# Row sums of reciprocals: inverse square roots and sums of squares in place of pairs, logarithms and TensorE sums

## The chip, the core and the metric

One core of one Trainium2 chip runs the kernel. The time is in device microseconds (us), from one execution of the program; a lower time is better. The kernel before has three runs: 167.90, 168.17 and 172.02 us, median 168.17 us. The profile is of one execution of its own, whose span from the first to the last instruction is 166.3 us.

Engines are named as the profile names them: PE is TensorE (PEld its weight loads), DVE is VectorE, ACT is ScalarE, POOL is GpSimd and SP is SyncE, which here only issues transfers.

## The reference

```python
"x": np.abs(np.random.randn(32, 512, 1024)).astype(np.float32) + 1e-6
...
def reference(x):
    return np.sum(1.0 / x, axis=-1).astype(np.float32)
```

There are 16,384 rows of 1,024 positive float32 numbers, 67.1 MB in all. Each row gives one number, the sum of the reciprocals of its elements.

## The kernel before

The rows are laid over 128 partitions, so that each partition has 128 rows of 1,024 elements. In what follows a "row" is one such row on all 128 partitions at once: 512 KB of input, 128 x 1024 elements. `ring` holds 40 rows in SBUF; row r lies in place r % 40. All loads go from SP's queue into `ring` (line 187). A load of n rows is one transfer, which lands as a whole for whoever waits for it, unless it wraps around the ring's end, where it is cut in two. SP issues the loads in order, and each waits until the rows that lay in its places before have been read for the last time.

The work uses 1/a + 1/b = (a + b) / (ab). A row is cut into two halves a and b of 512 elements. Their products go to `prod` (22 places of 512 elements):

- `P`, line 199: POOL multiplies the halves of one or two rows.
- `C` (line 209) and `V` (line 220): PE copies half b into a PSUM bank by a product with the identity matrix, and DVE multiplies half a by it. `W` (line 220 too) is the same product with both halves in SBUF.
- `L`, line 242, and `E`, line 251: ACT takes the logarithm of the product and then exp of minus that, which is 1/(ab). These two passes over half as many elements make about one pass over all of them. The result goes to a PSUM bank (`ps`) for some rows and stays in `prod` for others.
- `S`, line 232: for those others PE adds the halves, a + b, into a PSUM bank.
- `R`, line 267: DVE multiplies 1/(ab) by the sum, or by the whole row where PE made none, and sums the result along the row into `sums`. This is one instruction of 512 or of 1,024 elements and a short read of the accumulator.

The last two rows, 126 and 127, are loaded and worked on as four pieces of 512 elements.

The order of everything is a list written out by hand, `PLAN` (lines 38 to 73). A token is an operation, a row, a number of rows (`P0+2`), and a bank or place (`@3`); `D10` loads the next ten rows. The loop goes through the list and gives each token to its engine, so every engine has its own queue in the order of the list, and waits come only from the data. `note` drops waits that others imply. The first loads are `D2 D10 D14 D14`, and later ones become smaller down to single rows. The results leave in six small stores once the first 114 rows are done (line 289), and one store for the rest (line 291).

Of the kernel before, what the change touches and what calls it, by code (L numbers as in the profile page):

```python
# [11 lines left out]
def kernel(  # L12
# [5 lines left out]
    nc = tc.nc  # L18
    f32 = mybir.dt.float32
    P = 128  # L20
    D = 1024
    H = D // 2
    F = 128
    R = 40
    NP = 22
    LAST = F - 2
    DONE = 114
    S = float(2**17)

# [6 lines left out]
        D2 D10 D14 D14 P0+2 C3@3 S2@0 V3 P2 L0+2@0 C11@3 S3@1 E0+2@6 P4+2 V11 L2+2@2 R0 S6@2  # L39
        E2+2 R1 P6+2 L4+2@4 R2 R3 E4+2@6 S7@0 P8+2 L6+2@8 R4 S10@1 E6+2 R5 P10 L8+2@10 R6 R7  # L40
        S11@2 E8+2@6 L10+2@6 R8 E10+2 R9 D11 R10 R11 P12+2 C19@3 S14@0 V19 P14+2 L12+2@12
        S15@1 E12+2@6 S18@2 R12 P16+2 L14+2@16 R13 E14+2 R14 P18 L16+2@18 R15 S19@0 E16+2@6
        P20+2 L18+2@14 R16 S22@1 E18+2 R17 D9 P22+2 L20+2@20 R18 R19 E20+2@6 S23@2 P24+2
        L22+2@0 R20 E22+2 R21 L24+2@2 R22 R23 E24+2@6 P26 C27@3 R24 S26@0 P28+2 V27 R25 D7
        L26+2@4 C35@3 E26+2 S27@1 P30+2 V35 L28+2@8 R26 S30@2 R27 E28+2@6 P32+2 L30+2@10 R28
        S31@0 E30+2 R29 P34 L32+2@12 S34@1 R30 R31 E32+2@6 P36+2 S35@0 L34+2@6 R32 E34+2 R33
        D7 P38+2 S38@2 L36+2@16 R34 R35 E36+2@6 S39@1 P40+2 L38+2@18 R36 C43@3 E38+2 R37 D6
        S42@0 P42 L40+2@14 V43 R38 E40+2@6 P44+2 R39 S43@2 L42+2@20 R40 E42+2 S46@1 R41 D3
        P46+2 L44+2@0 R42 R43 E44+2@6 S47@0 P48+2 L46+2@2 R44 S50@2 E46+2 R45 P50 L48+2@4
        R46 C51@3 R47 E48+2@6 S51@1 P52+2 V51 R48 D6 L50+2@8 C59@3 E50+2 R49 P54+2 S54@0  # L50
        L52+2@10 V59 R50 E52+2@6 R51 S55@2 P56+2 L54+2@12 R52 E54+2 S58@1 R53 D5 P58
        L56+2@16 R54 R55 E56+2@6 S59@0 P60+2 L58+2@6 R56 S62@2 E58+2 R57 D4 P62+2 L60+2@14
        R58 R59 E60+2@6 S63@1 P64+2 L62+2@18 R60 S66@0 E62+2 R61 D4 P66 L64+2@20 R62 C67@3
        R63 E64+2@6 P68+2 S67@2 V67 R64 L66+2@0 S70@1 R65 D4 E66+2 P70+2 L68+2@2 R66 R67
        S71@0 E68+2@6 P72+2 L70+2@4 R68 D3 E70+2 R69 D2 C75@3 P74 L72+2@10 S74@2 R70 V75
        P76+2 E72+2@6 R71 S75@1 L74+2@8 R72 D2 E74+2 R73 D2 P80 S78@0 L76+2@12 R74 P81
        L80@16 R75 S79@2 E76+2@6 P78+2 L81@17 R76 D2 S81@1 E80@5 E81 R80 L78+2@6 W82 E78+2
        R81 R77 D1 D1 D1 D1 D1 P88 C85@6 S85@1 R78 P83 L88@18 V85 E88@7 R79 P84 S84@0
        L82+2@14 R88 E82+2@5 P86+2 L84+2@19 R82 D1 E84+2 R83 D1 D1 D1 C90@7 P91 L86+2@0
        S91@2 R85 P93 V90 E86+2@5 R84 P92 S90@1 L90+2@2 R87 L93@21 W89 L92@10 R86 D1 D1 D1  # L60
        D1 E93@7 P94 S97@0 E92@6 R93 E90+2 P97 S94@3 L89@11 R92 E89@7 P95 L97@8 R91 S95@4
        E97 R90 L94+2@4 W96 R97 P101 C99@6 L96@9 R89 E94+2 S100@0 P98 V99 E96@5 L101@12 R95
        P100 S99@1 L98@13 R96 E101@7 L99+2@16 R101 E98@6 P104 C103@5 R94 E99+2 S105@2 R98
        P102 L104@18 V103 E104@7 W105 L102+2@6 R100 P107+2 C106@6 L105@14 R104 E102+2@4
        S108@0 V106 E105 R102 L106+3@19 P109 S107@3 R103 P110 E106+3 R105 S106@4 R99 P111+2
        L109+2@0 R107 S112@1 R108 E109+2@6 R106 L111+2@10 P114 R109 S111@0 E111+2 R110 P113
        L114@15 R111 C115@7 P116 L113@2 R112 E114@6 V115 E113@5 S117@0 P117 R114 L116@3
        L115@8 P118 E116@7 R113 S118@1 E115@6 P119 L117+2@12 R116 E117+2 R115 P120 S120@2
        L119@9 R117 P121 L120@4 S121@3 R118 E119@7 E120 R119 P122 L121@5 S122@0 E121 R120
        P123 L122@18 R121 E122 W124 L123@6 R122 L124@7 W125 S125@1 E123@7 E124@6 R123 P126  # L70
        L125@14 P127 L126@16 S127@0 R124 E125 P128 L127@17 S128@2 E126@7 P129 R125 E127
        S129@3 L128@19 R126 L129@20 E128 R127 E129 R128 R129
    """.split()

    Ln = mybir.ActivationFunctionType.Ln
    Exp = mybir.ActivationFunctionType.Exp
# [10 lines left out]
            act_func_set_id=act_sets.index("natural_log_exp_and_others"),  # L87
# [6 lines left out]
    pspool = ctx.enter_context(  # L94
        tc.tile_pool(name="pspool", bufs=1, space=bass.MemoryType.PSUM)
    )
    ring = pool.tile([P, R, D], f32)
    prod = pool.tile([P, NP, H], f32)
    sums = pool.tile([P, F], f32)
    ident = pool.tile([P, P], f32)  # L100
    ps = pspool.tile([P, 8, H], f32)
    make_identity(nc, ident)

    def parse(tok):
        body, _, b = tok[1:].partition("@")
        r, _, n = body.partition("+")
        return tok[0], int(r), int(n or 1), int(b) if b else None

    ops = [parse(tok) for tok in PLAN]

    pslot = {r + j: b + j for op, r, n, b in ops if op == "L" for j in range(n)}

    def place(r):
        if r < LAST:
            return r, 0, H
        part, q = divmod(r - LAST, F - LAST)
        return LAST + q, part * H, H // 2

    def xs(r, h):
        q, at, w = place(r)  # L120
        return ring[:, q % R, at + h * w : at + (h + 1) * w]

    loaded = 0
    left = set(range(DONE))
    bank, copied, halves, summed = {}, {}, set(), set()

# [36 lines left out]
    def rows(r, n, h=None):  # L166
        spaces = []
        for q, at, w in (place(i) for i in range(r, r + n)):
            end = at + 2 * w
            if h is not None:  # L170
                at, end = at + h * w, at + (h + 1) * w
            spaces += [("row", q % R, i) for i in range(at, end, H // 2)]
        return spaces

    def slots(r, n):
        return [("slot", pslot[q]) for q in range(r, r + n)]

    with tc.manual_schedule():
        for op, r, n, b in ops:
            p = pslot.get(r)  # L180
            if op == "D":
                n, r = r, loaded
                while n:
                    q, at, w = place(r)
                    a = q % R
                    m = min(n, R - a, LAST - r) if r < LAST else 1
                    inst = nc.sync.dma_start(  # L187
                        out=ring[:, a : a + m, at : at + 2 * w],
                        in_=x_v[:, q : q + m, at : at + 2 * w],
                    )  # L190
                    note("SP", inst, writes=rows(r, m))
                    r, n = r + m, n - m
                loaded = r
            elif op == "P":
                while n:
                    q, at, w = place(r)
                    a, p = q % R, pslot[r]
                    m = min(n, R - a)
                    inst = nc.gpsimd.tensor_tensor(  # L199
                        out=prod[:, p : p + m, :w],  # L200
                        in0=ring[:, a : a + m, at : at + w],
                        in1=ring[:, a : a + m, at + w : at + 2 * w],
                        op=mult,
                    )
                    note("POOL", inst, rows(r, m), slots(r, m))
                    r, n = r + m, n - m
            elif op == "C":
                copied[r] = b
                inst = nc.tensor.matmul(  # L209
                    ps[:, b, : place(r)[2]],  # L210
                    lhsT=ident,
                    rhs=xs(r, 1),
                    start=True,
                    stop=True,
                )
                note("PE", inst, rows(r, 1, 1), [("bank", b)])
            elif op in "WV":
                w = place(r)[2]
                in1 = xs(r, 1) if op == "W" else ps[:, copied[r], :w]
                inst = nc.vector.tensor_tensor(  # L220
                    out=prod[:, p, :w], in0=xs(r, 0), in1=in1, op=mult
                )
                if op == "W":
                    read = rows(r, 1)
                else:
                    read = rows(r, 1, 0) + [("bank", copied[r])]
                note("DVE", inst, read, slots(r, 1))
            elif op == "S":
                bank[r] = b
                halves.add(r)  # L230
                for h in range(2):
                    inst = nc.tensor.matmul(  # L232
                        ps[:, b, : place(r)[2]],
                        lhsT=ident,
                        rhs=xs(r, h),
                        start=h == 0,
                        stop=h == 1,
# [84 lines left out]
```

## Time and profile before

| what | value |
|---|---|
| median of three runs | 168.17 us |
| profiled execution, span | 166.3 us |
| median less span | 1.87 us |
| busy, share of the span: PE, DVE, ACT, POOL | 80%, 77%, 80%, 77% |
| loads: bytes read, mean rate over the span | 67.11 MB, 404 GB/s |
| last store issued | 164.06 us |
| ACT's table load, once | 1.28 us |

The time of a run is the span and a little around it. The busy time of an engine says how much of the span it had an instruction running, not whether the kernel waited for it. The profile's chain shows, going back from the last instruction, what each step waited for. "Pitch" is used below for the distance from the start of one instruction to the start of the next on the same engine; where the next one doesn't wait for anything, the pitch is a little shorter than the duration of one, because instructions overlap at their ends.

### The profile page before, as it was taken

What the parts mean: (1) busy time and instruction counts of PE and PEld (TensorE: products, weight loads), DVE (VectorE), ACT (ScalarE), POOL (GpSimd) and SP (SyncE); (2) the same over time, 40 slices, a digit from 0 to 9 for tenths busy, and PEclk for the clock granted to TensorE, in tenths of its full rate; (3) what the DMA queues carried; (4) which work ended last, traced back from release to release, by engine and by line L of the source; (5) the groups of instructions that cost most, each with busy time, mean ns of one, the idle gap of its engine ahead of it and who ended that gap; (6) DMA issues with size and microseconds to landing.
All of it is one profiled execution on the core that took longest, in us unless ns stands there. A gap on an engine that the chain in (4) does not pass through costs nothing.

```text
span 166.3 us, 1348 instructions
## 1 busy us (share of the span) xinstructions
PE 132.5 (80%) x292; PEld 55.2 (33%) x292; DVE 128.3 (77%) x282; ACT 132.3 (80%) x157; POOL 128.2 (77%) x81
## 2 busy tenths in 40 slices
PE   0000799978855999999999999988699979989982
PEld 0000333333312444444343433324234424433351
DVE  0000119885787699898998898989899999999994
ACT  3040073949995899999799999996999999999992
POOL 1500795069995999999999999948977869999860
PEclk9999999999996999999999999999999999999999
DMA  5999999999998989999999999999999999999940
GB/s 189 536 394 394 441 441 441 441 441 441 441 441 349 509 368 446 430 417 438 441 434 434 406 426 446 429 424 424 414 437 437 414 410 428 410 409 410 400 139 4
DMA packets 5768, 67.26 MB, mean 404 GB/s; under 512 B 1536, under 2 KB 1536, under 8 KB 3200
## 3 DMA queue, kind: packets, MB, share of 16 engines
q1 hardware_dynamic: 5760, 67.18, 95.6%
q8 instruction: 2, 0.03, 0.1%
q14 instruction: 6, 0.05, 0.1%
HBM read 67.11 MB, written 0.07 MB: 404 GB/s over the span
## 4 chain that ended last, share of the span: by engine, by line
DMA 57%; PE 18%; ACT 8%; DVE 6%; POOL 6%; issue 3%; SPq 1%; ACTq 0%; POOLq 0%; DVEq 0%
DMA ring<-in_x_dram 57%; PE ps L232 15%; POOL prod L199 6%; ACT prod L242 4%; PE ps L209 3%; ACT ps L251 2%; DVE ring L267 2%; DVE prod L267 2%; ACT prod L251 2%; DVE prod L220 1%; SPq L187 1%; DVE sums L267 0%; ACTq L242 0%; POOLq L199 0%; DVEq L317 0%
## 5 line engine op out<-in xcount | busy, mean ns | idle before, releaser
L199 POOL TENSOR_TENSOR prod<-ring 128x1024 f32<-128x1024 f32 (+2 forms) x75 | 127.5, 1727 | 33.5 <-DMA ring<-in_x_dram 27.1
L232 PE MATMUL ps<-ring,ident 128*128 128x512 f32 (+1 forms) x260 | 116.9, 596 | 5.2 <-DVE sums L267 4.5
L242 ACT ACTIVATE prod<-prod 128x1024 f32<-128x1024 f32 (+2 forms) x78 | 68.5, 892 | 24.9 <-DVE prod L220 14.3
L267 DVE CUSTOM_DVE_ANT_1 ring<-ring,ps 128x1024 f32<-128x1024 f32 (+1 forms) x65 | 76.4, 1208 | 8.9 <-ACT ps L251 8.7
L232 PEld LDWEIGHTS ps<-ring,ident 128*128 128x128 f32 x260 | 49.2, 193 | 71.7 <-issue 51.6
L267 DVE CUSTOM_DVE_ANT_0 prod<-prod,ps 128x512 f32<-128x512 f32 (+1 forms) x63 | 40.9, 677 | 0.4 <-PE ps L232 0.4
L209 PE MATMUL ps<-ring,ident 128*128 128x512 f32 x32 | 19.3, 689 | 25.7 <-DMA ring<-in_x_dram 24.0
L251 ACT ACTIVATE ps<-prod 128x1024 f32<-128x1024 f32 (+2 forms) x41 | 34.1, 838 | 4.5 <-DVE sums L267 3.7
L251 ACT ACTIVATE prod<-prod 128x1024 f32<-128x1024 f32 (+3 forms) x37 | 34.4, 931 | 0.9
L220 DVE TENSOR_TENSOR prod<-ring,ps 128x512 f32<-128x512 f32 x16 | 10.9, 684 | 26.3 <-PE ps L209 26.3
L209 PEld LDWEIGHTS ps<-ring,ident 128*128 128x128 f32 x32 | 6.0, 213 | 36.0 <-issue 21.4
L267 DVE DVE_READ_ACCUMULATOR2_ANT sums<- 128x1 f32 x130 | 10.7, 82 | 0.0
L220 DVE TENSOR_TENSOR prod<-ring 128x512 f32<-128x512 f32 x6 | 4.1, 688 | 0.1
L84 ACT ACT_TABLE_LOAD x1 | 1.3, 1283 | 0.7 <-PEq L306 0.7
L267 DVE CUSTOM_DVE_ANT_0 prod<-prod,ps,sums 128x256 f32<-128x256 f32 x2 | 0.9, 475 | 0.0
masks.py:197 POOL MEMSET ident<- 128x128 f32 x1 | 0.2, 204 | 0.3 <-POOLq L306 0.3
masks.py:199 POOL TENSOR_SCALAR_AFFINE_SELECT ident<-ident 128x128 f32<-128x128 f32 x1 | 0.3, 292 | 0.1
L306 POOL MEMSET const-float32-0.0<- 128x1 f32 x1 | 0.1, 98 | 0.2 <-issue 0.2
L306 POOL MEMSET const-bfloat16-1.0<- 128x1 bf16 x1 | 0.1, 101 | 0.0
L306 POOL MEMSET const-uint8-127<- 128x1 uint8 x1 | 0.1, 101 | 0.0
L306 POOL MEMSET const-float32-1.0<- 128x1 f32 x1 | 0.1, 98 | 0.0
## 6 DMA issues: line engine op xcount, KB each, us to landing
ring<-in_x_dram SPq DMA_DIRECT2D x2, 7168.0 KB, 41.2
ring<-in_x_dram SPq DMA_DIRECT2D x2, 3584.0 KB, 29.3
ring<-in_x_dram SPq DMA_DIRECT2D x2, 3072.0 KB, 31.9
ring<-in_x_dram SPq DMA_DIRECT2D x3, 2048.0 KB, 34.0
ring<-in_x_dram SPq DMA_DIRECT2D x1, 5632.0 KB, 30.3
ring<-in_x_dram SPq DMA_DIRECT2D x5, 1024.0 KB, 31.8
ring<-in_x_dram SPq DMA_DIRECT2D x1, 5120.0 KB, 16.5
ring<-in_x_dram SPq DMA_DIRECT2D x1, 4608.0 KB, 30.7
```

Of the source, the lines that this page charges most:

```text
L84: nc.scalar.add_instruction(mybir.InstLoadActFuncSet(name=nc.get_next_instruction_name(), act_func_set_id=act_sets.index("natural_log_exp_ ...
L187: inst = nc.sync.dma_start(out=ring[:, a : a + m, at : at + 2 * w], in_=x_v[:, q : q + m, at : at + 2 * w],)
L199: inst = nc.gpsimd.tensor_tensor(out=prod[:, p : p + m, :w], in0=ring[:, a : a + m, at : at + w], in1=ring[:, a : a + m, at + w : at + 2 * w],
L209: inst = nc.tensor.matmul(ps[:, b, : place(r)[2]], lhsT=ident, rhs=xs(r, 1), start=True, stop=True,)
L220: inst = nc.vector.tensor_tensor(out=prod[:, p, :w], in0=xs(r, 0), in1=in1, op=mult)
L232: inst = nc.tensor.matmul(ps[:, b, : place(r)[2]], lhsT=ident, rhs=xs(r, h), start=h == 0, stop=h == 1,)
L242: inst = nc.scalar.activation(out=pg, in_=pg, func=Ln, scale=S)
L251: inst = nc.scalar.activation(out=rc, in_=pg, func=Exp, scale=-1.0)
L267: inst = nc.vector.tensor_tensor_reduce(out=row, in0=row, in1=other, scale=S, scalar=total if q in summed else 0.0, op0=mult, op1=add, acc ...
L306: nc = _bacc.Bacc("TRN2", target_bir_lowering=False, num_devices=1)
```

## The change

No halves, no pairs and no TensorE are left. ACT computes |x|^-1/2 of whole rows in place in `ring`, in instructions of up to four rows, and the row sum of 1/x is then the sum of the squares of these. The squares are summed in one of four ways:

- `B` (82 rows): VectorE's `bn_stats` on each half row of 512 elements. It gives the mean and a sum of squared deviations (`mean`, `var` in the code) of the even and of the odd elements. `K` later turns these into sums of squares for 32, 32, 32, 22 and 10 rows at once, in four short DVE instructions each.
- `Z` (19 units): ACT's Square with a sum along the row.
- `G` and `T` (26 units): POOL squares the row in place, up to three rows in one instruction, and DVE sums it with `tensor_reduce`.
- `Q` (2 rows): one DVE instruction multiplies the row by itself and sums.

A unit is a row; row 127 is two units of 512 elements, 127 (a `G`, `T` unit) and 128 (a `Z` unit), whose sums one last small DVE addition brings together. `ring` has 48 rows in place of 40. The first loads are of 16, 14 and 13 rows. The first store is of 118 rows, in six parts as before.

```diff
-    R = 40
-    NP = 22
-    LAST = F - 2
-    DONE = 114
-    S = float(2**17)
+    R = 48
+    PIECES = (512, 512)
+    DONE = 118
     PLAN = """
-        D2 D10 D14 D14 P0+2 C3@3 S2@0 V3 P2 L0+2@0 C11@3 S3@1 E0+2@6 P4+2 V11 L2+2@2 R0 S6@2
...
-        S129@3 L128@19 R126 L129@20 E128 R127 E129 R128 R129
+        D16 D14 D13 A0+4 A4+4 B0 Q1 B2 A8+4 G4+3 B3 A12+4 B8 Q9 B10 Z7 G12+3 T4+3 D10 Z15 A16+4
+        B11 A20+4 B16 T12+3 D9 A24+4 G20+3 B17 B18 B19 A28+2 B24 Z23 B25 G28+2 T20+3 D9 A30+4
+        B26 B27 A34+4 T28+2 B30 A38+4 B31 D9 B32 B33 A42 B34 Z37 B35 A43+4 K0+32 B36 D5 B38
+        A47+4 G44+2 B39 B40 B41 Z43 B42 D6 A51+2 T44+2 Z49 B46 D4 A53+4 B47 B48 B50 D4 A57+4 B51
+        B52 B54 Z53 G59 B55 D5 A61 Z60 B56 G61 B57 A62+4 B58 D3 T59 D2 T61 A66+4 G63 K32+32 B64
+        B65 Z62 G69 T63 D3 A70 B66 D3 G70 B67 B68 D2 A71+4 T69 T70 D2 A75+4 B71 B72 D2 B73 D1
+        A79 G75 B74 D1 A80+4 B76 B78 T75 D1 D1 Z77 D1 D1 B79 D1 D1 A84 B80 A85+4 B81 B83 B84 Z82
+        B85 A89+2 B86 A91+4 B87 B88 B89 A95+4 B90 B91 B92 Z96 B93 Z97 B94 A99+4 B95 B98 K64+32
+        A103 B99 A104+3 G103 B101 B102 Z100 T103 G106 A107+2 B104 B105 A109+3 G107 T106 B108
+        Z110 G109 T107 A112+3 B111 T109 A115+2 B112 B113 Z116 B114 A117+2 B115 A119+2 B117
+        K96+22 O0 A121 G119 B120 A122 B121 Z118 B122 A123 T119 A124 B123 A125 G124 A126 B125
+        A127 A128 K118+10 G127 T124 Z126 Z128 T127
     """.split()
...
-            act_func_set_id=act_sets.index("natural_log_exp_and_others"),
+            act_func_set_id=act_sets.index("abs_reciprocal_sqrt_and_small"),
...
+    stats = pool.tile([P, F, 2, 2, 3], f32)
+    part = pool.tile([P, F, 4], f32)
+    total = pool.tile([P, F], f32)
+    sums = pool.tile([P, F + 1], f32)
+    nc.gpsimd.memset(stats, 0.0)
+    nc.gpsimd.memset(sums, 0.0)
...
+            elif op == "A":
+                    inst = nc.scalar.activation(
+                        out=area(u, m), in_=area(u, m), func=Arsqrt, scale=1.0 - 2.0**-17)
...
+            elif op == "Z":
+                inst = nc.scalar.activation(
+                    out=area(u), in_=area(u), func=Square, accum_out=sums[:, c : c + 1])
...
+            elif op == "Q":
+                inst = nc.vector.tensor_tensor_reduce(
+                    out=row, in0=row, in1=row, scale=1.0, scalar=0.0,
+                    op0=mult, op1=add, accum_out=sums[:, u : u + 1])
...
+            elif op == "B":
+                for h in range(0, w, H):
+                    inst = nc.vector.bn_stats(
+                        out=stats[:, r, (at + h) // H],
+                        in_=ring[:, r % R, at + h : at + min(h + H, w)])
...
+            elif op == "G":
+                    inst = nc.gpsimd.tensor_tensor(out=row, in0=row, in1=row, op=mult)
...
+            elif op == "T":
+                    inst = nc.vector.tensor_reduce(
+                        out=sums[:, u : u + m], in_=area(u, m), axis=mybir.AxisListType.X, op=add)
...
+            elif op == "K":
+                nc.vector.tensor_tensor(out=tmp, in0=mean, in1=mean, op=mult)
+                nc.vector.scalar_tensor_tensor(
+                    out=tmp, in0=tmp, scalar=float(H // 2), in1=var, op0=mult, op1=add)
+                nc.vector.tensor_reduce(out=total[:, u : u + n], in_=part[:, u : u + n], axis=mybir.AxisListType.X, op=add)
+                nc.vector.tensor_tensor(
+                    out=sums[:, u : u + n], in0=sums[:, u : u + n], in1=total[:, u : u + n], op=add)
+            elif op == "O":
+                for c in range(0, DONE, DONE // 6):
+                    store(c, min(c + DONE // 6, DONE))
+        nc.vector.tensor_tensor(
+            out=sums[:, F - 1 : F], in0=sums[:, F - 1 : F], in1=sums[:, F : F + 1], op=add)
+        store(DONE, F)
```

More of the change, by code (lines that the diff above doesn't have):

```diff
@@ L7 @@
 from concourse.hw_specs import get_activation_tables
-from concourse.masks import make_identity
 @with_exitstack
@@ L23 @@
     F = 128
-    R = 40
-    NP = 22
-    LAST = F - 2
-    DONE = 114
-    S = float(2**17)
-    PLAN = """
-        D2 D10 D14 D14 P0+2 C3@3 S2@0 V3 P2 L0+2@0 C11@3 S3@1 E0+2@6 P4+2 V11 L2+2@2 R0 S6@2
[L40 to L71, printed above, removed]
-        S129@3 L128@19 R126 L129@20 E128 R127 E129 R128 R129
@@ L73 @@
     """.split()
-    Ln = mybir.ActivationFunctionType.Ln
-    Exp = mybir.ActivationFunctionType.Exp
+    Arsqrt = mybir.ActivationFunctionType.Abs_reciprocal_sqrt
+    Square = mybir.ActivationFunctionType.Square
     mult = mybir.AluOpType.mult
@@ L93, with place, area @@
     pool = ctx.enter_context(tc.tile_pool(name="pool", bufs=1))
-    pspool = ctx.enter_context(
-        tc.tile_pool(name="pspool", bufs=1, space=bass.MemoryType.PSUM)
-    )
     ring = pool.tile([P, R, D], f32)
[L98 to L102, printed above, removed]
-    def parse(tok):
[L105 to L125, printed above, removed]
+    stats = pool.tile([P, F, 2, 2, 3], f32)
[4 more added lines that the diff above has]
+    nc.gpsimd.memset(sums, 0.0)
+    def parse(tok):
+        r, _, n = tok[1:].partition("+")
+        return tok[0], int(r), int(n or 1)
+    def place(u):
+        k = u - (F - 1)
+        if k < 0:
+            return u, 0, D
+        return F - 1, sum(PIECES[:k]), PIECES[k]
+    def area(u, n=1):
+        r, at, w = place(u)
+        return ring[:, r % R : r % R + n, at : at + w]
     history = {}
@@ L164, in note, with rows @@
                 )
-    def rows(r, n, h=None):
+    def rows(u, n=1):
         spaces = []
[L168 to L172, printed above, removed]
-        return spaces
-    def slots(r, n):
-        return [("slot", pslot[q]) for q in range(r, r + n)]
+        for r, at, w in (place(i) for i in range(u, u + n)):
+            spaces += [("row", r % R, i) for i in range(at, at + w, 128)]
+        return spaces
@@ L178, with store @@
+    loaded = 0
+    left = set(range(DONE))
+    def store(lo, hi):
+        nc.sync.dma_start(out=out_v[:, lo:hi], in_=sums[:, lo:hi])
     with tc.manual_schedule():
-        for op, r, n, b in ops:
-            p = pslot.get(r)
+        for op, u, n in (parse(tok) for tok in PLAN):
             if op == "D":
-                n, r = r, loaded
+                n, u = u, loaded
                 while n:
-                    q, at, w = place(r)
-                    a = q % R
-                    m = min(n, R - a, LAST - r) if r < LAST else 1
+                    r, at, w = place(u)
+                    m = min(n, R - r % R, F - 1 - u) if u < F - 1 else 1
@@ L187 @@
                     inst = nc.sync.dma_start(
-                        out=ring[:, a : a + m, at : at + 2 * w],
-                        in_=x_v[:, q : q + m, at : at + 2 * w],
-                    )
[L191 to L194, printed above, removed]
+                        out=area(u, m), in_=x_v[:, r : r + m, at : at + w]
+                    )
+                    note("SP", inst, writes=rows(u, m))
@@ L195 @@
+                    u, n = u + m, n - m
+                loaded = u
+            elif op == "A":
                 while n:
[L196 to L203, printed above, removed]
-                    )
@@ L205 @@
[L205 to L214, printed above, removed]
-                )
[L216 to L237, printed above, removed]
-                    )
-                    note("PE", inst, rows(r, 1, h), [("bank", b)])
-            elif op == "L":
-                pg = prod[:, p : p + n, : place(r)[2]]
-                inst = nc.scalar.activation(out=pg, in_=pg, func=Ln, scale=S)
-                note("ACT", inst, writes=slots(r, n))
-            elif op == "E":
-                pg = prod[:, p : p + n, : place(r)[2]]
-                rc = pg
-                if b is not None:
-                    rc = ps[:, b : b + n, : place(r)[2]]
-                    for j in range(n):
-                        bank[r + j] = b + j
-                inst = nc.scalar.activation(out=rc, in_=pg, func=Exp, scale=-1.0)
-                if b is None:
-                    note("ACT", inst, writes=slots(r, n))
-                else:
-                    banks = [("bank", b + j) for j in range(n)]
-                    note("ACT", inst, slots(r, n), banks)
-            elif op == "R":
-                q, at, w = place(r)
-                other = ps[:, bank[r], :w]
-                if r in halves:
-                    row = prod[:, p, :w]
-                else:
-                    row = ring[:, q % R, at : at + 2 * w]
-                    row = row.rearrange("p (h e) -> p h e", h=2)
-                    other = other.unsqueeze(1).to_broadcast([P, 2, w])
-                total = sums[:, q : q + 1]
@@ new lines @@
+                    m = min(n, R - place(u)[0] % R)
+                    inst = nc.scalar.activation(
+                        out=area(u, m),
+                        in_=area(u, m),
+                        func=Arsqrt,
+                        scale=1.0 - 2.0**-17,
+                    )
+                    note("ACT", inst, writes=rows(u, m))
+                    u, n = u + m, n - m
+            elif op == "Z":
+                c = u - (F - 1) if u >= F else 0
+                c = F if c else u
+                inst = nc.scalar.activation(
+                    out=area(u), in_=area(u), func=Square, accum_out=sums[:, c : c + 1]
+                )
+                note("ACT", inst, writes=rows(u))
+            elif op == "Q":
+                row = area(u)
@@ L269 @@
                     in0=row,
-                    in1=other,
-                    scale=S,
-                    scalar=total if q in summed else 0.0,
+                    in1=row,
+                    scale=1.0,
+                    scalar=0.0,
                     op0=mult,
                     op1=add,
-                    accum_out=total,
+                    accum_out=sums[:, u : u + 1],
                 )
-                summed.add(q)
-                note(
-                    "DVE",
-                    inst,
-                    [("bank", bank[r])],
-                    slots(r, 1) if r in halves else rows(r, 1),
-                )
@@ L285 @@
-                left.discard(r)
-                if not left:
-                    for c in range(0, DONE, DONE // 6):
-                        part = slice(c, min(c + DONE // 6, DONE))
-                        nc.sync.dma_start(out=out_v[:, part], in_=sums[:, part])
-                    left.add(-1)
-        nc.sync.dma_start(out=out_v[:, DONE:], in_=sums[:, DONE:])
+                note("DVE", inst, writes=rows(u))
+            elif op == "B":
+                r, at, w = place(u)
+                for h in range(0, w, H):
+                    inst = nc.vector.bn_stats(
+                        out=stats[:, r, (at + h) // H],
+                        in_=ring[:, r % R, at + h : at + min(h + H, w)],
+                    )
+                    half = [("row", r % R, i) for i in range(at + h, at + min(h + H, w), 128)]
+                    note("DVE", inst, reads=half)
+            elif op == "G":
+                while n:
+                    m = min(n, R - u % R)
+                    row = area(u, m)
+                    inst = nc.gpsimd.tensor_tensor(out=row, in0=row, in1=row, op=mult)
+                    note("POOL", inst, writes=rows(u, m))
+                    u, n = u + m, n - m
+            elif op == "T":
+                while n:
+                    m = min(n, R - u % R)
+                    inst = nc.vector.tensor_reduce(
+                        out=sums[:, u : u + m],
+                        in_=area(u, m),
+                        axis=mybir.AxisListType.X,
+                        op=add,
+                    )
+                    note("DVE", inst, reads=rows(u, m))
+                    u, n = u + m, n - m
+            elif op == "K":
+                mean = stats[:, u : u + n, :, :, 1].rearrange("p f h e -> p (f h e)")
+                var = stats[:, u : u + n, :, :, 2].rearrange("p f h e -> p (f h e)")
+                tmp = part[:, u : u + n].rearrange("p f q -> p (f q)")
+                nc.vector.tensor_tensor(out=tmp, in0=mean, in1=mean, op=mult)
+                nc.vector.scalar_tensor_tensor(
+                    out=tmp, in0=tmp, scalar=float(H // 2), in1=var, op0=mult, op1=add
+                )
+                nc.vector.tensor_reduce(
+                    out=total[:, u : u + n],
+                    in_=part[:, u : u + n],
+                    axis=mybir.AxisListType.X,
+                    op=add,
+                )
+                nc.vector.tensor_tensor(
+                    out=sums[:, u : u + n],
+                    in0=sums[:, u : u + n],
+                    in1=total[:, u : u + n],
+                    op=add,
+                )
+            elif op == "O":
+                for c in range(0, DONE, DONE // 6):
+                    store(c, min(c + DONE // 6, DONE))
@@ L295 @@
+        nc.vector.tensor_tensor(
+            out=sums[:, F - 1 : F],
+            in0=sums[:, F - 1 : F],
+            in1=sums[:, F : F + 1],
+            op=add,
+        )
+        store(DONE, F)
 _INS = ['x']
```

## The prediction

> **What bounds the kernel now.** I first read the page's strips over the span, because they tell stages apart where the totals (every engine near 80%) do not.
>
> ```profile
> DMA  5999999999998989999999999999999999999940
> GB/s 189 536 394 394 441 441 441 441 441 441 441 441 349 509 368 446 430 417 438 441 434 434 406 426 446 429 424 424 414 437 437 414 410 428 410 409 410 400 139 4
> ```
>
> The loads run from the first slices to the 38th at 400 to 440 GB/s with no gap. So I went to the chain for the moments at which loads are seen to land, and for the end:
>
> ```profile
> 2.11 49.45 DMA ring<-in_x_dram
> ...
> 147.18 10.17 DMA ring<-in_x_dram
> 157.34 0.02 issue
> ...
> 163.63 0.39 DVE prod L267
> 164.02 0.01 DVEq L317
> ```
>
> The first transfer starts at 2.1; the fourth load (40 rows in all) has landed at 51.56, row 124 (125 rows) at 157.34. The timeline shows the second load (12 rows) landing at 17.75, when POOL's second instruction starts. So a row takes (51.56 - 17.75) / 28 = 1.207 us at first, in large transfers, and (157.34 - 51.56) / 85 = 1.244 later, in small ones. SP's own waits show that the loads are not held up:
>
> ```profile
> SPq L187 <- DVE sums L267: 87.8, 14, 32.1
> ```
>
> SP waits long for free places, but the page gives a median of some 30 us from issue to landing, so transfers queue behind each other all the while. In stretches of the end the rate falls from 348 GB/s at 158.5-159 to 44 at 160.5-161 and 1 after it: the loads end between 160 and 161. Behind them lies a tail of work to 164.03, then the last store to 166.3 (2.27 us). The bound is the stream, then a tail of some 3 us.
>
> **The stream after.** It moves the same bytes, again in large transfers first. Transfers of one and two rows cover 16 rows by the new list, 21 by the old; at 1.207 against 1.244 these five are worth 0.2 us, which I leave out. The first load is now of 16 rows, and all wait for it: 17.75 + 4 x 1.207 = 22.6. The second (30 rows) lands at 39.5, the third (43 rows) at 51.56 + 3 x 1.207 = 55.2. The last piece lands at 160 to 161 as now. Compute thus starts 17 us later than today's first product (5.66), and what matters is whether DVE and ACT catch up.
>
> **DVE, step by step.** What goes are PE, the products, and 130 `R`. What comes is priced by pitch:
>
> ```profile
> 145.88 1.22 DVE L267 CUSTOM_DVE_ANT_1 ring<-ring,ps 128x1024 f32<-128x1024 f32 x1
> 147.02 0.08 DVE L267 DVE_READ_ACCUMULATOR2_ANT sums<- 128x1 f32 x1
> ...
> 156.00 0.68 DVE L267 CUSTOM_DVE_ANT_0 prod<-prod,ps 128x512 f32<-128x512 f32 x1
> 156.60 0.08 DVE L267 DVE_READ_ACCUMULATOR2_ANT sums<- 128x1 f32 x1
> ```
>
> Start to start, 1,024 elements take 1.14 us and 512 take 0.605: 1.045 ns per element and 0.07 us. No row shows `bn_stats`. Below, it could not beat the 0.535 that 512 elements cost without the fixed part. Above, the nearest rows are the last three 256-element sums of `R`: one follows the other after 0.34 us, and after 0.40 where it needs the other's result, so a flush at its end costs 0.06: 0.67. Two full passes would be 1.2. I take 0.605, the row of the same size. `tensor_reduce` goes by the same line (from nothing fixed to 0.06 more for each of its 18, 1 us either way).
>
> - `B`: 82 x 2 x 0.605 = 99.2.
> - `T`: 25.5 rows x 1.07 + 18 x 0.07 = 28.5.
> - `Q`: 2 x 1.14 = 2.3.
> - `K`: 128 elements at 0.07 + 0.13 = 0.2, three of them and a shorter one: 0.7, four times, and 0.45 for the last: 3.2. Nothing hides them, since they stand in DVE's queue.
>
> The sum is 133.2, against 128.3 busy now. Its start needs ACT's first instruction:
>
> ```profile
> L242 ACT ACTIVATE prod<-prod 128x1024 f32<-128x1024 f32 x50 | 52.3, 1046 | 23.3 <-DVE prod L220 14.3 <-POOL prod L199 8.8
> L242 ACT ACTIVATE prod<-prod 128x256 f32<-128x256 f32 x4 | 1.5, 399 | 0.0
> L242 ACT ACTIVATE prod<-prod 128x1536 f32<-128x1536 f32 x1 | 1.5, 1487 | 0.2 <-POOL prod L199 0.2
> ```
>
> The slope is (1487 - 399) / 1280 = 0.85 ns, so four rows take 3.66 us, and 3.56 as a pitch (two independent ones of 512 take 1.13 together, 0.10 less than twice 0.617). `B0` starts at 22.6 + 3.66 = 26.3. `B0 Q1 B2 B3` last to 31.1; `B8` waits for the third `A`, 33.4 (2.3 idle). `B8 Q9 B10 T4+3 B11` last to 41.5 (POOL's `G4+3`, 3 x 2.36 from 29.8, is ready at 36.9). `B16` waits for the second load and its `A`: 39.5 + 3.66 = 43.2 (1.7 idle). From there the lag behind the loads is paid back, at 1.03 us of DVE a row against 1.24 of stream, and DVE has no reason to wait: 26.3 + 133.2 + 2.3 + 1.7 = **163.5**.
>
> **ACT.** `A`: 131,072 x 0.85 ns + 49 x 0.08 = 115.3, about what `L` and `E` cost. `Z`: 18.5 rows x 0.87 + 19 x 0.08 = 17.6, and a read of ACT's accumulator that no row shows: from nothing to 0.36 (the shortest ACT instruction); I take 0.13, nearer to DVE's 0.08: 2.5. In sum 135.4, which from 22.6 with waits of 0.4 (second load) and 2.1 (third) ends at 160.5. So ACT has a reserve of 3 us, and near the end single `A` follow the loads. There the last piece lands at up to 161.1, then `A128` 0.53, `Z126` 0.97 + 0.13 and `Z128` 0.53 + 0.13 in ACT's queue: 163.4. `Z126` also waits for `K118+10`, because both write that stretch of `sums`. By the list above, DVE has `T124`, `T127` (1.75) after `K118+10`, so `Z126` could start at 161.8 and the end be 163.6.
>
> **POOL** squares 25.5 rows x 2.36 = 60 us, half of today's 128; only `G127` (1.28 after `A127`) is near the end, hidden by `T124`. The two memsets at its start, the table load (1.28) and SP's issues lie in the 22 us before the first row; without that cover each would delay only a start. The ring's 48 places against an 18-row lag leave 30 rows for transfers in flight, as much as today's 40 with their shorter lag; the six stores are behind all loads in SP's queue, as now.
>
> **The sum.** Last DVE work 163.5 to 163.6, the last addition 0.1, the store and end 2.27: span 166.0, against 166.3. The profiled span stands 1.87 below the median of the runs, which I keep: **167.9 us**, no change. 2% (3.4 us) is about what a measurement of this kernel can tell from none.
>
> **A rule weighed.** All six products with both inputs in SBUF (`W`) stand outside POOL's instructions but for 0.13 us at the last, while POOL is busy 77% of the span; whether they would wait, no row tells. The Trainium skill, "SBUF — State Buffer", section "Who interferes with whom", says that a DVE instruction with two SBUF inputs and a POOL instruction that reads SBUF lock each other out for a whole instruction, and that one with a single input does not. That no run here shows. Such waits, as a mechanism of this kernel, would hold `Q` and `K`, not `B` and `T`: `Q9` stands at 34.6 in `G4+3`, which ends at 36.9, and 1.7 of these 2.3 us are the wait at `B16` anyway; `K32+32`, `K96+22` and `K118+10` may each meet a one-row `G`, mean delay half of 2.36 at most. That is 0.6 to 3 us: 168.5 to 171.
>
> **Rivals.**
> 1. *Statistics cost more than a pass* (slower). DVE has no idle time after 43, so 164 instructions carry every excess straight to the end: +0.02 us each is +3.3 (171.2, the point from which it is slower by 2%), +0.065 is +10.7 (178.6), two passes +98 (266). For it: two moments of two interleaved sets come out of each instruction, and six numbers are written. Against: no simple DVE row of one width differs from another by over 0.01 in pitch. Chance 0.22.
> 2. *ACT or the lock adds a little*: `Z` at 0.36 adds 4.4 to ACT, past its reserve by 1.4, or `Q` and `K` wait for POOL as priced above: 168.5 to 171. Chance 0.18, within 2%.
> 3. *The loads get faster.* If the whole stream kept 1.207, it would land at 17.75 + 116 x 1.207 = 157.8, and with ACT's tail of 2.3 and cheap statistics the end is 160.1, the time 164.3. Against: the small transfers, whose 1.244 it is, hardly become fewer. Chance 0.06, faster.
> 4. *The program is not what it says*: if Square is not in the loaded table, each run of `Z` costs two table loads of 1.28: 19 x 2.57 = 49, most of it past ACT's reserve: about 214. Chance 0.03.
>
> **Numbers.** Forecast 0.51 (166.5 to 169), rivals as above. Faster by 2%: 0.06; within: 0.51 + 0.18 = 0.69; slower: 0.25. The range goes down to 166, where DVE is cheap and the tail waits for loads alone (160 + 2.3 + 2.27 + 1.87 = 166.4), and up to 176, where `bn_stats` costs 0.655; the unknown upper ends beyond it hold about 0.1.
>
> **What would show it.** Right: first `ACT` at 22.6; DVE idle about 4 us between 26 and 164; `bn_stats` with a pitch near 0.605; `tensor_reduce` near 3.3 for three rows; loads ending at 160 to 161. Wrong: a `bn_stats` pitch over 0.625, with SP waiting for `B` rows and loads ending later; a second table load; DVE waiting while `G` runs; ACT's waits for loads gone at the end. The forecast is also wrong if the first load of 16 rows, larger than any in this trace, lands much later than 22.6.

## The result

The changed kernel takes 171.97 us (median of four runs, 171.83 to 172.55). Its time over that of the kernel before is 1.024, with a 95% interval of 1.022 to 1.026: slower, where no change was forecast. (One of the four runs of the kernel before, at 172.02 us, was a slow one and is not counted in this ratio.) The span of the profiled execution is 169.8 us against 166.3.

The page of the changed kernel, its busy times, its chain and its costliest groups (busy us and mean ns of one behind the first bar, idle time before behind the second):

```profile
DVE 136.2 (80%) x207; ACT 135.8 (80%) x88; POOL 48.7 (29%) x24
...
GB/s 247 494 401 355 479 432 432 432 432 401 439 452 376 434 439 440 443 425 434 452 434 443 417 394 437 428 423 400 450 437 408 429 423 413 419 410 410 213 0 1
...
DVE 72%; DMA 23%; ACT 2%; issue 1%; SPq 0%; DVEq 0%
...
L181 DVE BATCH_NORM_STATS2 stats<-ring 128x6 f32<-128x512 f32 x164 | 99.3, 680 | 30.3 <-ACT ring L150 30.3
...
L209 DVE TENSOR_TENSOR part<-stats 128x128 f32<-128x128 f32 (+2 forms) x5 | 2.5, 502 | 0.1
L219 DVE TENSOR_TENSOR sums<-sums,total 128x32 f32<-128x32 f32 (+2 forms) x5 | 2.2, 438 | 0.2
```

The stream is nearly as full as before (396 GB/s over the span for 404) and ends, as before, between 160 and 161 us. The chain has moved: 57% of it were loads, now 72% is DVE. The statistics cost what a plain pass costs (0.68 us for 512 elements, as a product of 512 did before). The means of the rows for lines 209 and 219 are strange: instructions of at most 128 and of 32 elements take 502 and 438 ns in the mean.

The chain shows that from 43.67 us on it never leaves DVE. Here are the last step of `K0+32`, the whole of `K64+32`, and the end (start us, length us, what):

```profile
70.06 0.19 DVE sums L219
...
134.61 0.24 DVE part L209
134.85 0.02 issue
134.87 0.35 DVE part L210
135.22 0.02 issue
135.24 0.30 DVE total L213
135.54 0.02 issue
135.56 1.45 DVE sums L219
...
165.02 0.18 DVE sums L219
...
165.29 1.82 DVE sums L197 x2
```

The four steps of a `K` stand one behind the other with a short gap between them, and the last one, an addition of 32 elements, takes 1.45 us here, but 0.19 at 70.06 (and 0.18 at 165.02, where it has 10 elements). The timelines of POOL and of DVE at this place say why:

```profile
135.01 1.95 POOL L191 TENSOR_TENSOR ring<-ring 128x1024 f32<-128x1024 f32 x1 [24.92 <-ACT ring L150]
```

```profile
135.24 0.29 DVE L213 TENSOR_REDUCE total<-part 128x32 f32<-128x128 f32 x1
135.56 1.45 DVE L219 TENSOR_TENSOR sums<-sums,total 128x32 f32<-128x32 f32 x1
136.94 0.68 DVE L181 BATCH_NORM_STATS2 stats<-ring 128x6 f32<-128x512 f32 x1
```

POOL squares a row from 135.01 to 136.96. The sum of `K` (two inputs in SBUF) starts in it and ends at 137.01, right behind it. The reduction at 135.24, with one input, is as long as ever. The same is seen at `Q9` (1.72 in place of 1.21), in `K32+32` (a first step of 1.09 in place of 0.32) and in `K96+22` (0.57 in place of 0.28). The delays within `K` are 1.26 + 0.77 + 0.29 = 2.3 us; that of `Q9`, 0.5, falls before a wait of DVE and is hidden there.

Theory: `K` takes DVE far longer than forecast and puts its end off, half of the excess by waits for POOL's squares, half because each step of a `K` needs the result of the one before. Rivals: statistics and sums on DVE are too much work by themselves; the late start (first ACT instruction at 23.10) is never made up; smaller transfers slow the stream.

### The profile page after: what moved, and what is told of

Same layout as the page of the kernel before. It is cut to its first block, busy times and chain, and to the rows that moved or that the text cites. A ratio compares the mean times of both kernels' runs of the same rounds, so it can differ in the third digit from the quotient of the medians.

```text
span 169.8 us, 437 instructions
## 1 busy us (share of the span) xinstructions
DVE 136.2 (80%) x207; ACT 135.8 (80%) x88; POOL 48.7 (29%) x24
## 4 chain that ended last, share of the span: by engine, by line
DVE 72%; DMA 23%; ACT 2%; issue 1%; SPq 0%; DVEq 0%
DVE stats L181 53%; DMA ring<-in_x_dram 23%; DVE sums L197 15%; ACT ring L150 2%; DVE part L209 1%; DVE sums L219 1%; DVE part L210 1%; DVE total L213 1%; SPq L141 0%; DVE sums L228 0%; DVEq L228 0%; DVEq L197 0%; DVEq L219 0%
## 5 line engine op out<-in xcount | busy, mean ns | idle before, releaser
L150 ACT ACTIVATE ring<-ring 128x4096 f32<-128x4096 f32 (+4 forms) x49 | 115.8, 2419 | 27.2 <-DMA ring<-in_x_dram 27.0
L181 DVE BATCH_NORM_STATS2 stats<-ring 128x6 f32<-128x512 f32 x164 | 99.3, 680 | 30.3 <-ACT ring L150 30.3
L191 POOL TENSOR_TENSOR ring<-ring 128x1024 f32<-128x1024 f32 (+3 forms) x18 | 47.0, 2609 | 113.5 <-ACT ring L150 113.5
L197 DVE TENSOR_REDUCE sums<-ring 128x1 f32<-128x1024 f32 (+3 forms) x18 | 29.4, 1649 | 0.1
L161 ACT ACTIVATE ring<-ring 128x1024 f32<-128x1024 f32 (+1 forms) x19 | 19.4, 1021 | 3.2 <-DVE sums L219 3.2
L161 ACT ACTIVATION_READ_ACCUMULATOR ring<-ring 128x1 f32 x19 | 3.5, 186 | 0.0
L167 DVE CUSTOM_DVE_ANT_0 ring<-ring 128x1024 f32<-128x1024 f32 x2 | 2.9, 1466 | 0.0
L209 DVE TENSOR_TENSOR part<-stats 128x128 f32<-128x128 f32 (+2 forms) x5 | 2.5, 502 | 0.1
L219 DVE TENSOR_TENSOR sums<-sums,total 128x32 f32<-128x32 f32 (+2 forms) x5 | 2.2, 438 | 0.2
L167 DVE DVE_READ_ACCUMULATOR2_ANT sums<- 128x1 f32 x2 | 0.2, 80 | 0.0
```

The lines of the kernel that those rows point to most:

```text
L150: inst = nc.scalar.activation(out=area(u, m), in_=area(u, m), func=Arsqrt, scale=1.0 - 2.0**-17,)
L161: inst = nc.scalar.activation(out=area(u), in_=area(u), func=Square, accum_out=sums[:, c : c + 1])
L167: inst = nc.vector.tensor_tensor_reduce(out=row, in0=row, in1=row, scale=1.0, scalar=0.0, op0=mult, op1=add, accum_out=sums[:, u : u + 1],)
L181: inst = nc.vector.bn_stats(out=stats[:, r, (at + h) // H], in_=ring[:, r % R, at + h : at + min(h + H, w)],)
L191: inst = nc.gpsimd.tensor_tensor(out=row, in0=row, in1=row, op=mult)
L197: inst = nc.vector.tensor_reduce(out=sums[:, u : u + m], in_=area(u, m), axis=mybir.AxisListType.X, op=add,)
```

## The experiments

**No POOL.** The squares of POOL become statistics, and three units `Q` (63, 124 and 127, whose sums come after or beside their `K`).

```diff
-        ... A8+4 G4+3 B3 A12+4 B8 Q9 B10 Z7 G12+3 T4+3 D10 ...
+        ... A8+4 B3 A12+4 B8 Q9 B10 Z7 B4 B5 B6 D10 ...
```

> All POOL squares are gone: 23 of their 26 units become statistics (B), units 63, 124 and 127 become Q. Theory 1 (DVE instructions with two SBUF inputs wait for POOL's running instruction): the squares and sums of K fall to 0.32 and 0.19 us each time, all five K together from 7.95 to about 5.5 us, and Q9 from 1.72 to 1.21; DVE pays 2.1 us more for B in place of T, so the time falls only a little, to 171 to 171.5. Theory 2 (K is as dear as it is by itself, by its strided reads and its waits): K stays at 7.95 and the time rises by 2 us to 174.

Measured: 171.29 us, 1.019 [1.017, 1.021] of the kernel before. DVE's groups:

```profile
L180 DVE BATCH_NORM_STATS2 stats<-ring 128x6 f32<-128x512 f32 x210 | 125.5, 678 | 30.3 <-ACT ring L149 30.3
...
L208 DVE TENSOR_TENSOR part<-stats 128x128 f32<-128x128 f32 x3 | 1.0, 322 | 0.0
...
L218 DVE TENSOR_TENSOR sums<-sums,total 128x32 f32<-128x32 f32 x3 | 0.6, 192 | 0.2
```

The steps of `K` are at 0.32 and 0.19 us each time, as theory 1 has it: by pitch the five `K` take 5.5 us together, in place of 7.9. The time falls by 0.7 us although `B` in place of `T` costs DVE more. So the means of 502 and 438 ns are not the price of strided reads; `K` waited for POOL. The 5.5 us that are left are still more than the 3.2 that were forecast.

**One `K`.** Three of the five are merged into the fourth.

```diff
-        ... K0+32 ... K32+32 ... K64+32 ... K96+22 ...
+        ... K0+118 ...
```

> K0+32, K32+32, K64+32 and K96+22 become one K0+118 at the place of the last of them. Theory (the tail of DVE's queue is work that never finds a gap, so every us of K counts): 7.0 us of K become 2.4 to 3.5, DVE's last work would move from 167.4 to about 163, and ACT's own last rows (A128 ends at 162.1, then two squares of 1.04 and 0.7) set the end at about 164: 168.2 to 169.0. Rival (the loads and the stored tail set the end, K is hidden): 171.5 to 172.

Measured: 171.96 us, 1.023 [1.021, 1.024]: a miss; nothing is gained. DVE's own waits in the timeline and the merged `K`:

```profile
104.51 7.21 DVE L181 BATCH_NORM_STATS2 stats<-ring 128x6 f32<-128x512 f32 x12 [1.48 <-ACT ring L150]
133.88 3.66 DVE L181 BATCH_NORM_STATS2 stats<-ring 128x6 f32<-128x512 f32 x6 [0.85 <-ACT ring L150]
```

```profile
152.90 0.80 DVE L209 TENSOR_TENSOR part<-stats 128x472 f32<-128x472 f32 x1
153.43 2.04 POOL L191 TENSOR_TENSOR ring<-ring 128x1024 f32<-128x1024 f32 x1 [8.46 <-ACT ring L150]
153.74 2.39 DVE L210 SCALAR_TENSOR_TENSOR part<-part,stats 128x472 f32<-128x472 f32 x1
156.16 0.65 DVE L213 TENSOR_REDUCE total<-part 128x118 f32<-128x472 f32 x1
156.84 0.28 DVE L219 TENSOR_TENSOR sums<-sums,total 128x118 f32<-128x118 f32 x1
```

The 5.6 us of the first three `K` (1.14, 2.00 and 2.42 by the changed kernel's timeline) are gone, but DVE then catches up with ACT at 104 and at 134 and waits there for 2.3 us, since ACT follows the loads. And the merged `K` stands in the last 15 us with 4.1 us in place of 1.3, 1.6 of them a wait for POOL's square at 153.43. So "every us of `K` counts" was wrong: the early `K` are in part hidden by waits that would come anyway, while behind the merged `K` DVE finds no wait in which to make it up.

**The head.** First only the first load is cut, then all three.

```diff
-        D16 D14 D13 A0+4 ...
+        D12 D4 D14 D13 A0+4 ...
```

> The first load of 16 rows is cut into 12 and 4, so the first ACT instruction starts at 17.8 in place of 23.1. Theory (the wait for the second load at 40.0 takes back what an early start gives): DVE finishes its first 16 rows earlier, waits longer at B16, and the time stays at 171.6 to 172.2. Rival (the late start is paid in full at the end): 4 to 5 us less, 167 to 168.

```diff
-        D16 D14 D13 A0+4 ...
+        D12 D4 D8 D6 D8 D5 A0+4 ...
```

> All three first loads are cut in two (12+4, 8+6, 8+5), so that neither ACT nor DVE waits for the last row of a large one. Theory (DVE's start plus its unbroken work sets the end): DVE gains up to 5 us, then ACT's own tail and the loads end at about 164: 168 to 169.5. Rival (the start is no matter, or smaller loads cost as much in the stream): 171.5 or more.

Measured: 171.77 us (1.022 [1.020, 1.023]) and 170.83 us (1.016 [1.015, 1.018]). With the first load cut, the timeline shows the early start taken back at the second load:

```profile
18.28 14.14 ACT L150 ACTIVATE ring<-ring 128x4096 f32<-128x4096 f32 x4 [16.27 <-DMA ring<-in_x_dram]
...
40.10 10.63 ACT L150 ACTIVATE ring<-ring 128x4096 f32<-128x4096 f32 x3 [5.61 <-DMA ring<-in_x_dram]
43.75 1.29 DVE L181 BATCH_NORM_STATS2 stats<-ring 128x6 f32<-128x512 f32 x2 [6.23 <-ACT ring L150]
```

With all three cut, the gain is 1.1 us, less than expected. DVE starts its 17th row 5.6 us earlier (38.03 in place of 43.67), loses most of that in waits for ACT (2.15 at 83, 0.94 at 94, 1.51 at 105), and then meets POOL in its tail:

```profile
154.70 1.89 POOL L191 TENSOR_TENSOR ring<-ring 128x1024 f32<-128x1024 f32 x1 [9.21 <-ACT ring L150]
154.88 1.75 DVE L219 TENSOR_TENSOR sums<-sums,total 128x22 f32<-128x22 f32 x1
```

An addition of 22 elements takes 1.75 us. The late start is not the main thing that the change loses by; a lead at 40 us is worth little at 160.

**The wait for POOL, at scale.** Every `B` becomes a `Q`, whose two inputs are both the row in SBUF, so that `K` goes; POOL's squares stay. And the same with POOL filling the rows in place of squaring them; in that kernel the sums of 26 units are wrong, since their squares are left out.

```diff
-        ... A0+4 A4+4 B0 Q1 B2 A8+4 G4+3 B3 ...
+        ... A0+4 A4+4 Q0 Q1 Q2 A8+4 G4+3 Q3 ...
```

> Every B becomes a Q (one DVE instruction with the row as both inputs, 1.14 us in place of 1.19), K goes, POOL squares and T stay. If two-input DVE instructions wait for POOL's whole instruction: 18 POOL instructions of 48.7 us in sum block DVE for 25 to 38 us of it, DVE ends at 180 to 192, the time is 183 to 197. If they do not wait: DVE's work falls by 12 us, ACT's tail sets the end at 164, the time is 168 to 169.

```diff
-                    inst = nc.gpsimd.tensor_tensor(out=row, in0=row, in1=row, op=mult)
+                    inst = nc.gpsimd.memset(row, 1.0)
```

> e5_allq with POOL's squares replaced by POOL filling the same rows with a constant, which reads nothing (the sums of 26 units are then wrong). If any running POOL instruction holds a two-input DVE instruction up, the fills of about 0.9 us a row hold DVE for 10 to 20 us and Q's mean stays above 1.3 us; if only POOL instructions that read SBUF do, Q's mean is 1.21 and the time 168 to 169.

Measured: 194.64 us (1.157 [1.155, 1.159]) with squares and 168.20 us (one run) with fills. The group of the `Q` in the first and in the second:

```profile
L166 DVE CUSTOM_DVE_ANT_0 ring<-ring 128x1024 f32<-128x1024 f32 x84 | 133.6, 1647 | 29.1 <-ACT ring L149 29.1
```

```profile
L166 DVE CUSTOM_DVE_ANT_0 ring<-ring 128x1024 f32<-128x1024 f32 x84 | 97.8, 1220 | 37.2 <-ACT ring L149 37.1
```

With squares the 84 `Q` take 84 x (1.647 - 1.22) = 36 us more in sum of durations, the longest of them 6.3 us; with fills none: 22 of the `Q` run beside a fill, and the longest of these takes 1.23 us. So a DVE instruction with two inputs in SBUF waits for a POOL instruction that reads SBUF, and not for one that only writes. This is what the Trainium skill, "SBUF — State Buffer", section "Who interferes with whom", states; here it is worth 26 us between two kernels that differ in one instruction of POOL.

**Neither `K` nor POOL.** All of DVE's and POOL's rows become `Q`:

```diff
-        D16 D14 D13 A0+4 A4+4 B0 Q1 B2 A8+4 G4+3 B3 A12+4 B8 Q9 B10 Z7 G12+3 T4+3 D10 ...
+        D16 D14 D13 A0+4 A4+4 Q0 Q1 Q2 A8+4 Q3 A12+4 Q8 Q9 Q10 Z7 Q4 Q5 Q6 D10 ...
```

> All of DVE's and POOL's rows become Q on DVE; neither POOL, nor statistics, nor K is left. DVE has 110 rows x 1.14 = 125 us from 26.8, with 4 us of waits it could end at 156, so it only follows the loads. ACT's last rows end at 162.1 as now, then its two squares 1.04 and 0.7, the last addition 0.2: 164.1, the time 168 to 169. If it stays near 172, neither K nor POOL is what DVE's tail costs.

**No `K` alone.** Statistics, POOL's squares and `T` stay; only `K` is left out, so the sums of the 82 `B` rows are missing from the output.

```diff
-        ... K0+32 ... K32+32 ... K64+32 ... K96+22 ... K118+10 ...
```

> The changed kernel without any K: the sums of squares of the 82 B rows are left out of the output. If K (7.95 us of DVE, with its waits for POOL) is what the tail costs, ACT's last rows and squares set the end at about 164: 168.2 to 169. If the statistics and the POOL squares hold DVE by themselves, it stays above 170.5.

Measured: 168.47 us (1.001 [1.000, 1.002]) and 168.34 us (1.0015 [1.0006, 1.0025]). Without `K` the whole loss is gone, and the chain's end is the one that was forecast for ACT's tail. The kernel without `K`:

```profile
156.36 4.82 ACT ring L149 x6
161.18 0.95 ACT ring L160
...
162.22 0.62 ACT ring L160 x2
...
162.97 0.16 DVE sums L227
```

So `K` with its waits is what makes the change slower: the statistics, the squares and the late start are all still in the kernel without `K`, and do not make it slower by themselves. Nor is it the stream, which ends in the changed kernel where it did before (144 GB/s from 159 to 160 and 27 in the next us, for 146 and 71).

**Better versions.** The last kernels keep `Q` on DVE and a few `Z` on ACT, with new lists. The first has loads of 2, 6 and then 8 rows, and every seventh row up to 117 as `Z`; the second the changed kernel's loads with the same rule. In both the `Q` of the last half row adds onto the sum of the half before it.

```diff
+        D2 D6 D8 D8 D8 D8 D8 A0+2 Q0 Q1 A2+4 Q2 Q3 Q4 A6+2 Z5 Q6 Q7 D8 A8+4 Q8 ...
...
+        A119+2 Z117 Q119 Q120 O0 A121+2 Q121 Q122 A123 Q123 A124 Q124 ... A128 Q128
...
-                    scalar=0.0,
+                    scalar=sums[:, F - 1 : F] if u >= F else 0.0,
```

> Inverse square roots on ACT, all sums by Q on DVE except every seventh row by Z, no POOL, no statistics, no K; the last two half rows go to DVE, the second adding onto the first; loads of 2, 6, then 8 rows, and small ones only at the end, so compute follows the loads from the start. ACT has 129 us of work and DVE 128 in 155 us of stream, so both only follow. The loads end at about 159.8 (by the packet rates of the runs, 0.4 us less stream than the changed kernel's); then an ACT piece of 0.61 and a Q of 0.69: DVE ends at 161.3 to 162, the span is 163.7 to 164.5, the time 165.8 to 166.6, which is 0.986 to 0.991 of the kernel before. If small loads are what the stream loses by, it ends at 157.5 and the time is 163.5.

```diff
+        D16 D14 D13 A0+4 Q0 Q1 Q2 Q3 A4+4 Q4 Q6 Q7 D10 A8+4 Z5 Q8 Q9 Q10 Q11 A12+4 Q13 ...
```

> The same as e7_best with the changed kernel's loads (16, 14, 13, 10 and so on), all else by the same rules. If the late start no longer matters once DVE and ACT have reserves, it catches up before the end and the time is that of e7_best within 0.5 us. If the late start matters still, it is 1 to 3 us longer.

Measured: 171.93 us (1.023 [1.022, 1.025]) and 169.78 us (1.011 [1.009, 1.012]), both worse than expected, the first by 5 us; and the second is not longer than the first, as either of its expectations had it, but 2.2 us shorter. The timeline of the first at the end:

```profile
153.64 1.23 DVE L165 CUSTOM_DVE_ANT_0 ring<-ring 128x1024 f32<-128x1024 f32 x1 [0.29 <-ACT ring L148]
...
167.09 0.75 DVE L165 CUSTOM_DVE_ANT_0 ring<-ring,sums 128x512 f32<-128x512 f32 x1
```

DVE waits for the last time at 153.64, for ACT's instruction over rows 115 to 118, and works off a backlog until 167.85, one `Q` every 1.145 us, while ACT is through with its last piece at 163.1. From the list, no `Z` is left to ACT after row 117, so DVE has all the sums of the end alone. In neither kernel is DVE short of time over the whole span: after its first instruction it waits for ACT 17 times for 30.7 us in the first, and 9 times for 9.8 us in the second. It is short of it in the last 15 us.

The last one has first loads of 14 rows, later ones that become smaller down to single rows, and `Z` at rows 107, 111, 116, 124 and 127 in the tail:

```diff
+        D14 D14 D14 A0+4 Q0 Q1 Q2 Q3 A4+4 Q6 Q7 A8+4 Z4 Z5 Q9 Q10 D12 A12+2 Z8 Z11 Q12 ...
...
+        O0 A120 Q120 A121+2 Q121 Q122 A123 Q123 A124 A125 Z124 Q125 A126 Q126 A127 A128 Z127 ...
```

> e6_allq_nopool's kinds of work (inverse roots on ACT, Q on DVE, a few Z on ACT, no POOL, no statistics, no K) with first loads of 14 rows, later ones falling evenly from 12 to 1, and the Z spread so that ACT and DVE enter the last 15 rows with no backlog. The chain ACT - Q then follows the loads, which end at 159.7 to 160.3: DVE's end is 162 to 163 in place of e6's 163.8, the time 166.8 to 168.0. If each single-row A and Q of the tail is already as dense as the stream allows, it stays at 168.5.

Measured: 167.96 us, 0.9988 [0.9979, 0.9997] of the kernel before. It is the best version here, and by 0.1% only. Loads and `Z` were changed together, so no run says which of them helped. What bounds it now is argued and not shown: the loads still move at 91 GB/s from 159 to 160 (with loads of 8 rows, in the first of the three, at 201 from 158 to 159 and 37 after that), and an `A`, a `Q`, the last addition and the store (2.4 us) come behind them. But ACT too has no wait for a load after 141.04 in this kernel, so its own work may bound the end as well.

## Why the prediction was wrong

It failed at one term of DVE's sum: "`K`: 128 elements at 0.07 + 0.13 = 0.2, three of them and a shorter one: 0.7, four times, and 0.45 for the last: 3.2". By pitch in the changed kernel's timeline the five take 1.14, 2.00, 2.42, 1.31 and 1.00: 7.9 us. The end of DVE's work before the last addition moved from the 163.5 of the sum to 167.1:

| term | forecast | measured |
|---|---|---|
| start of `B0` | 26.3 | 26.8 |
| waits of DVE after it | 4.0 | 2.13 + 1.33 = 3.5 |
| `B` (164) | 99.2 | 97.9 (34 in a row take 20.18) |
| `T` | 28.5 | 28.4 |
| `Q` | 2.3 | 2.8 |
| `K` | 3.2 | 7.9 |

The measured terms add up to 167.2, the start of the last addition. `K` was mis-sized for two reasons. The first, 2.3 us, is the wait for POOL. The prediction weighed it under "A rule weighed" and in rival 2, "mean delay half of 2.36 at most", for three of the `K`, and then gave it 0.18 together with a dearer `Z`; three did meet POOL. The second, the other 2.4 us, no part of the prediction had: I priced the steps by the pitch of instructions that don't need each other. Each step of `K` needs the one before, so each costs its full duration and a gap (0.32, 0.34, 0.29 and 0.19, 1.14 us with the gaps, in place of 0.7). No run changes this half alone; it is what is left of the excess in the kernel without POOL, 5.5 us for 3.2. The durations there are close to an estimate from rows of the kernel before (0.68 us at 512 and 1.22 at 1,024 elements give 0.28 at 128), so strided reads have little part in it. The timeline of the kernel before had a sign of it, 0.40 us in place of 0.34 for a 256-element sum that needs the one before; at 0.06 for each of 20 steps that is 1.2 us, half of the 2.4. I used it as a bound for `bn_stats` and not for `K`. The two reasons together take the time past the 168.5 to 171 of rival 2. That the stated range, up to 176, holds 171.97 is luck: its upper part was there for a dearer `bn_stats`, which did not come.

One reading under "A rule weighed" is a little off: the `W` that overlaps POOL by 0.13 us is the one at 157.37, the last but one. It took 0.69 us, and the other five 0.68 to 0.69.

What was right:

- The stream: it ends between 160 and 161 (27 GB/s is left in that stretch), and single loads land as worked out (first ACT instruction at 23.10 for 22.6, the second wait over at 40.02 for 39.5).
- `bn_stats` costs what a plain pass over 512 elements does (0.594 against 0.605). Rival 1, which was given most weight of those that end slower, did not happen; its sign came about by another mechanism.
- One table load of 1.28 us, so rival 4 fell, and rival 3 too: the loads of the changed kernel still move at 144 GB/s in the stretch from 159 to 160.
- `Z126` waits for `K118+10`: by 3.15 us, since `K118+10` ends at 165.2 in place of 161.8.
- ACT's tail as the next bound, at 163.4 to 163.6: the kernel without `K` ends its last addition at 163.1.

That the 4.7 us too little at `K` came out as 3.6 us at DVE's end is mostly the cheaper `B`. That taking `K` out gives 3.6 us and not 7.9 is ACT's tail, which is late next.

## What to carry to other kernels

Price a DVE instruction that needs the result of the one before by its full duration and the gap, as the steps of `K` had it here (1.14 us for four, in place of 0.7), and not by the pitch of independent ones. Look at which DVE instructions have two inputs in SBUF, and put them where POOL reads nothing, or give POOL something else: a small addition waited up to 1.6 us for a square that it had nothing to do with. And in a kernel that a stream bounds, count the work of each engine that stands behind the last loads: of the 5.6 us of `K` that were taken out earlier, 2.3 were lost again in waits for what follows the stream, and what stood in the last 15 us found no wait to hide in.

## What was not expected of the hardware

- POOL squares a row in place in 1.89 us (three rows in 5.31), while its product of two different halves, of the same number of results, took 2.36 us in the kernel before. That is a fifth less; the square has the same row as both inputs and as output, and no run says which of these it is.
- Both sides wait: beside `Q` the mean of POOL's one-row squares went from 1.90 to 2.68 us.
- ACT's read of its accumulator takes 0.186 us, but lies mostly under the next instruction: a `Z` and its read have a pitch of 1.04 us, while an `A` of one row has 0.95.
- The first load of 16 rows moves pieces of 64 KB; it landed within 0.5 us of what the rate of the 14-row loads in the kernel before gave (first ACT instruction at 23.10 for 22.6).
